# Weight splits and a scaling of X move from GpSimd to VectorE, and three groups of instructions are pinned in program order

## The chip, the cores and the metric

The kernel runs on one core of one Trainium2 chip. A core has TensorE (matmul, and its weight load), VectorE, ScalarE, GpSimd and SyncE; profiles call them PE and PEld, DVE, ACT, POOL and SP. The metric is the device time of one execution in microseconds, as the median of several runs; lower is better.

## The reference: what is computed

A sequence of 256 tokens of width 1024 goes through three transformer layers, all in float32:

```python
# layer 1: short convolution and gated linear attention, then a convolved gated MLP
x = x + rmsnorm(mixer(rmsnorm(x)) @ w_out);  x = x + rmsnorm(conv_mlp(rmsnorm(x)))
# layer 2: two kinds of attention, a SwiGLU, a per-layer gate
x = layer_norm(ALPHA * x + fox_sb_mixer(x));  x = layer_norm(ALPHA * x + swiglu(x))
x = x + sigmoid(x @ ple_gate[0]) * (p[0] @ ple_proj[0])
# layer 3: sliding-window attention, a mixture of experts, a per-layer gate
x = layer_norm(ALPHA * x + swa_mixer(x))
x = layer_norm(ALPHA * x + moe_swiglu(x))     # 8 experts, each token in its best 2
x = x + sigmoid(x @ ple_gate[1]) * (p[1] @ ple_proj[1])
```

The mixture computes router logits, takes the softmax of the two best, and adds up each expert's output with these weights. An expert has a 1024 x 7168 gate-and-up matrix and a 3584 x 1024 down matrix, 44 MB together, and the eight of them are most of what is read.

## The kernel before, in words

**Weights as a stream.** All weights are packed on the host into granules of 128 x 2048 float32 (1 MB), listed in the order of their use (`queue`, from L290), and loaded by SP into a ring of buffers called `raw`: 5 at first, 16 in the experts. The ring moves on when a granule is used up (`finish`, `load`). Some entries of the queue aren't weights: `("rep", 6)` holds the gain and the bias of the norm ahead of the experts, and while `main.hold` stands at its place in the queue, no buffer from that one on is loaded again.

**Splits.** For precision most weights are used as two fp32r parts. Each granule is split by halves of 128 x 1024 (`Stream.split`, L389): ScalarE rounds `raw` to `wh` (L405), and `wl = raw - wh` is done on VectorE (L409) or, for the halves named in `main.aside`, on GpSimd (L407). `ASIDE` (L31) names two halves behind each of six weight matrices: those are split while a norm is running. Three matmuls (`mm3`, L462 to L464) then make the product. Four halves can be live (`HALVES`), and splitting runs three halves ahead of use (`AHEAD`).

**The norms between the stages.** Each projection that ends a stage adds into `X` (tokens on partitions, two tiles `tt` of 128), takes the statistics, raises the variance to -1/2 on GpSimd (`rsqrt`, L617), and writes `X` in two halves `u`: L736 after the RMS norms of layer 1, L1062 and L1068 after a LayerNorm. Then TensorE turns `X` around (`turn_in`, L666) for the next stage. In a LayerNorm, `ordered[0]` makes `keep` pin what is traced between the first and the second token tile in program order, splits on VectorE among them.

**Who sets the order.** The program is traced in one order, and a scheduler then orders each engine's queue by its own estimate of when inputs are ready; `tc.keep_in_program_order(ins)` pins an instruction behind everything traced on its engine so far. `put_off` holds functions that are traced later: `flush_once` runs those waiting, and is called after each granule's matmuls, so that what is put off lands between two granules.

**The experts.** A router (L1557 to L1572) gives each token its places, `ranks` (L1584) each token's slot within an expert. `gates` (L1624) then computes the two gates of a token and calls `sort` (L1648), which orders the experts by their number of tokens and hands that order to SP as registers (L1669): in the order of the work, crowded experts alternate with those of few tokens. `in_order` puts the gates and slots into that order. `gates` also scales X by the gain and adds the bias, on GpSimd (L1644, L1645), and lets `main.hold` go. Expert 0 doesn't depend on the order. Its input comes from `gather` (L1707): matmuls of X with a one-hot of the slots (L1715), evacuated by ScalarE and VectorE by halves of four blocks (L1742, L1744) and split (L1745, L1746).

An expert's 3584 hidden columns go in seven blocks. `up(j)` takes four granules, `down(j - 1)` two, in turn. `Expert` works on 128 tokens with split weights, 12 matmuls a granule; `ExpertOfFew` on 64 with the weights as they are (L1791, L1823), which are neither rounded nor subtracted. There `gated` applies Silu and multiplies (L1799, L1800), and `turn` transposes the product (L1806) and copies it (L1808) for `down(j)`:

```python
                def turn():
                    pt = bank()
                    for m in range(2):
                        TE.transpose(pt[:, m * P:m * P + P], sg[:, m * P:m * P + P], ident)
                    ht = mh.tile([P, 2, P], F32, name="ht", tag="hh")
                    V.tensor_copy(ht, pt[:, :T].rearrange("p (a b) -> p a b", a=2))
```

In program order `gated` is traced behind the first granule of `down(j - 1)` and `turn` behind the second; in the last block of each half of the experts (`soon`) each is one granule earlier.

Of the kernel before, what the change touches and what calls it, by code (L numbers as in the profile page):

```python
# [28 lines left out]
GW = 2048  # L29

ASIDE = dict(w_out=(0, 2), w_down=(1, 3), ab_out=(0, 2), ffn_dn=(1, 3), c_out=(1, 2), moe=(0, 1))  # L31


# [190 lines left out]
def block_kernel(ctx: ExitStack, tc: tile.TileContext, A: dict, out: bass.AP):  # L224
# [94 lines left out]
    class Stream:  # L319
# [4 lines left out]
        def __init__(self, queue, pool, depth):  # L324
# [17 lines left out]
            self.fine = set()  # L342
            self.aside = set()

# [44 lines left out]
        def split(self, upto):  # L389
            while len(self.parts) < min(upto, self.stop):  # L390
                n = len(self.parts)
                i, h = self.halves[n]
                if i in self.as_is:
                    self.parts.append(None)
                    continue
                if self.live >= HALVES:
                    break
                self.live += 1
                self.load()
                hi = hlp.tile([P, GW // 2], F32R, name="wh")  # L400
                lo = hlp.tile([P, GW // 2], F32R, name="wl")
                step = GW // 8 if i in self.fine else GW // 2
                for c in range(0, GW // 2, step):
                    raw = self.raws[i][:, h * GW // 2 + c:h * GW // 2 + c + step]
                    S.activation(hi[:, c:c + step], raw, AF.Copy)  # L405
                    if n in self.aside:
                        nc.gpsimd.tensor_tensor(lo[:, c:c + step], raw, hi[:, c:c + step], op=ALU.subtract)  # L407
                    else:
                        keep(V.tensor_tensor(lo[:, c:c + step], raw, hi[:, c:c + step], op=ALU.subtract))  # L409
                self.parts.append((hi, lo))  # L410
                if n + 1 == len(self.halves) or self.halves[n + 1][0] != i:
                    self.finish(i)
                self.load()
# [36 lines left out]
    main = Stream(queue, rawp, RAW)  # L450
    for n, key in enumerate(queue[1:], 1):
        if queue[n - 1][0] != key[0] and queue[n - 1][0] in ASIDE and queue[n - 1][0] != "moe":
            main.aside |= {main.first[n] + i for i in ASIDE[queue[n - 1][0]]}
    main.fine |= {0, 1}
    main.aside |= {main.first[queue.index(("ple_p", 1))] + i for i in ASIDE["moe"]}
    stream = [main]
# [1164 lines left out]
    with tc.tile_pool(name="moe", bufs=1, side="right") as mp, tc.tile_pool(name="moe2", bufs=2, side="right") as mw, \  # L1621
            tc.tile_pool(name="moeh", bufs=2, side="right") as mh:
        Y = mp.tile([P, 2, D], F32, name="Y")
        def gates():  # L1624
            oh1, oh2, t8 = (mp.tile([P, 2, 8], F32, name=n) for n in ("oh1", "oh2", "t8"))
            m1, m2, ga = (mp.tile([P, 2, 1], F32, name=n) for n in ("m1", "m2", "ga"))
            for oh, m, n in ((oh1, m1, 0.0), (oh2, m2, 1.0)):
                V.tensor_scalar(oh, place, n, None, op0=ALU.is_equal)
                V.tensor_tensor(t8, oh, lg, op=ALU.mult)
# [12 lines left out]
            gain = main.other(("rep", 6)).rearrange("p (n d) -> p n d", n=2)  # L1642
            for tt in range(2):
                nc.gpsimd.tensor_tensor(X[:, tt], X[:, tt], gain[:, 0], op=ALU.mult)  # L1644
                nc.gpsimd.tensor_tensor(X[:, tt], X[:, tt], gain[:, 1], op=ALU.add)  # L1645
            main.hold = len(queue)

        def sort():  # L1648
# [5 lines left out]
            def by8(v):  # L1654
                return C(v).rearrange("p (a b) -> p a b", a=8)
            V.tensor_copy(t8, cnt)
            V.memset(t8[:, 0:1], 1000.0)
# [17 lines left out]
            V.tensor_copy(cnti, pos[:, 0:1])  # L1675
            V.tensor_scalar(slot, sel8, -1000.0, 1000.0, op0=ALU.mult, op1=ALU.add)
            V.tensor_tensor(slot, slot, rank, op=ALU.add)
# [79 lines left out]
        class ExpertOfFew:  # L1757
# [24 lines left out]
            def up(self, j, before=iter(()), soon=False):  # L1782
# [20 lines left out]
                def turn():  # L1803
                    pt = bank()
                    for m in range(2):
                        TE.transpose(pt[:, m * P:m * P + P], sg[:, m * P:m * P + P], ident)  # L1806
                    ht = mh.tile([P, 2, P], F32, name="ht", tag="hh")
# [266 lines left out]
```

## Time and profile before

| | |
|---|---|
| time, median of 3 runs | 1705.84 us (1705.81 to 1706.9) |
| profiled execution: its time | 1706.26 us |
| profiled execution: span of the trace | 1704.5 us, mean granted TensorE clock 0.985 |
| VectorE busy | 1065.2 us (62%), 1516 instructions |
| ScalarE busy | 841.1 us (49%), 1159 instructions |
| GpSimd busy | 52.9 us (3%), 36 instructions |
| DMA | 487.76 MB, mean 286 GB/s |

How to read it: a profile is of one execution, and its own time stands 1.76 us above its span, since the span runs from the first to the last instruction. Shares of busy time are means over stages that differ: the first 780 us are layers 1, 2 and the attention of layer 3, the experts run to about 1660 us, the rest is the last norm and gate. In a timeline a line merges neighbouring instructions of one kind (x4 is four of them), and the bracket at its end says how long the engine stood idle before it and what ended that.

### The profile page before, as it was taken

How to read it: one execution, taken by the hardware profiler on the slowest of the kernel's cores; microseconds unless marked ns; L12 is line 12 of the kernel's file. 1: busy time of each engine (PE TensorE's matmuls, PEld its weight loads, DVE VectorE, ACT ScalarE, POOL GpSimd, SP SyncE). 2: the span in 40 equal slices, each digit the busy share in tenths (PEclk: the TensorE clock that was granted, in tenths of full speed). 3: DMA queues.
4: the chain of work that ended last, by engine and by line, in shares of the span. 5: the costliest groups of instructions: out<-in, count | busy, mean ns of one | idle time of the engine just before them, and what ended most of it. 6: DMA issues, size and time to landing. Idle time of an engine off the chain costs nothing. (4 is left out here: it accounts for less than half of the span.)

```text
span 1704.5 us, 23510 instructions
## 1 busy us (share of the span) xinstructions
PE 1637.6 (96%) x9029; PEld 1223.9 (72%) x9029; DVE 1065.2 (62%) x1516; ACT 841.1 (49%) x1159; POOL 52.9 (3%) x36
## 2 busy tenths in 40 slices
PE   8999999899899999997999999999799999999997
PEld 7988998798699987966886357863378734787325
DVE  6578996566755557678996139961189712897107
ACT  7346665446454534564774037740177601686013
POOL 0000000100100001003000000000000000000001
PEclk9999999999999999997999999999999999999999
DMA  8344554543255554834998999999999899999990
GB/s 321 114 171 171 188 192 170 195 173 124 103 200 177 182 185 165 355 114 150 371 364 328 420 420 420 420 392 421 418 369 420 324 421 420 420 420 393 420 390 25
DMA packets 69668, 487.76 MB, mean 286 GB/s; under 512 B 7739, under 2 KB 8763, under 8 KB 11308
## 3 DMA queue, kind: packets, MB, share of 16 engines
q1 hardware_dynamic: 68572, 484.10, 72.1%
q10 hardware_dynamic: 896, 1.82, 0.3%
q8 instruction: 72, 1.18, 0.3%
q0 software_dynamic: 80, 0.26, 0.1%
q14 instruction: 48, 0.39, 0.1%
HBM read 485.11 MB, written 1.05 MB: 285 GB/s over the span
## 5 line engine op out<-in xcount | busy, mean ns | idle before, releaser
L409 DVE TENSOR_TENSOR wl<-raw,wh 128x1024 fp32r<-128x1024 f32 (+1 forms) x570 | 679.5, 1201 | 229.7 <-ACT wh L405 224.3
L405 ACT ACTIVATE wh<-raw 128x1024 fp32r<-128x1024 f32 (+1 forms) x582 | 602.5, 1042 | 360.9 <-PE mm L464 176.7
L462 PE MATMUL mm<-a_l,wh 128*128 128x256 f32 x1008 | 284.5, 283 | 0.0
L463 PE MATMUL mm<-a_h,wh 128*128 128x256 f32 x1008 | 281.4, 279 | 0.0
L464 PE MATMUL mm<-a_h,wl 128*128 128x256 f32 x1008 | 281.1, 279 | 0.0
L1791 PE MATMUL mm<-raw,xgf 128*64 128x512 f32 x896 | 200.4, 595 | 0.0
L462 PEld LDWEIGHTS mm<-a_l,wh 128*128 128x128 f32 x1008 | 189.3, 188 | 2.8 <-issue 1.7
L463 PEld LDWEIGHTS mm<-a_h,wh 128*128 128x128 f32 x1008 | 188.9, 187 | 0.7 <-issue 0.5
L464 PEld LDWEIGHTS mm<-a_h,wl 128*128 128x128 f32 x1008 | 189.1, 188 | 0.0
L462 PE MATMUL mm<-wl,xg 128*128 128x512 f32 x448 | 181.4, 405 | 6.5 <-ACT xg L1745 6.5
L464 PE MATMUL mm<-wh,xg 128*128 128x512 f32 x448 | 177.2, 396 | 0.9 <-DVE xg L1746 0.9
L463 PE MATMUL mm<-wh,xg 128*128 128x512 f32 x448 | 177.6, 396 | 0.0
L1791 PEld LDWEIGHTS mm<-raw,xgf 128*64 128x64 f32 x896 | 62.1, 137 | 118.9 <-issue 117.2
L598 ACT ACTIVATE sgf<-mm 128x256 f32<-128x256 f32 x28 | 10.7, 384 | 234.4 <-PE mm L1791 234.4
L1800 DVE TENSOR_TENSOR sgf<-sgf,mm 128x256 f32<-128x256 f32 x28 | 11.8, 420 | 176.5 <-ACT sgf L598 176.5
L462 PEld LDWEIGHTS mm<-wl,xg 128*128 128x128 f32 x448 | 84.5, 189 | 28.6 <-ACT xg L1745 6.7
L1823 PE MATMUL at<-raw,ht 128*64 128x512 f32 x448 | 102.5, 598 | 0.0
L464 PEld LDWEIGHTS mm<-wh,xg 128*128 128x128 f32 x448 | 84.3, 188 | 21.7 <-DVE xg L1746 1.1
L463 PEld LDWEIGHTS mm<-wh,xg 128*128 128x128 f32 x448 | 84.6, 189 | 18.7
L463 PE MATMUL at<-wh,hh 128*128 128x512 f32 x224 | 89.1, 398 | 0.0
L462 PE MATMUL at<-wl,hh 128*128 128x512 f32 x224 | 89.1, 398 | 0.0
L464 PE MATMUL at<-wh,hl 128*128 128x512 f32 x224 | 87.9, 393 | 0.0
(409 smaller groups left out, 2071.8 us busy)
## 6 DMA issues: line engine op xcount, KB each, us to landing
raw<-in_moe_gu_dram SPq DMA_DIRECT2D x224, 1024.0 KB, 12.4
raw<-in_moe_dn_dram SPq DMA_DIRECT2D x112, 1024.0 KB, 12.5
raw<-in_w_up_dram SPq DMA_DIRECT2D x22, 1024.0 KB, 4.8
raw<-in_ffn_gu_dram SPq DMA_DIRECT2D x22, 1024.0 KB, 4.8
raw<-in_w_in_dram SPq DMA_DIRECT2D x12, 1024.0 KB, 10.5
raw<-in_ab_in_dram SPq DMA_DIRECT2D x12, 1024.0 KB, 4.8
raw<-in_w_down_dram SPq DMA_DIRECT2D x10, 1024.0 KB, 4.8
raw<-in_ffn_dn_dram SPq DMA_DIRECT2D x10, 1024.0 KB, 4.8
```

What stands on the lines that cost most here:

```text
L405: S.activation(hi[:, c:c + step], raw, AF.Copy)
L409: keep(V.tensor_tensor(lo[:, c:c + step], raw, hi[:, c:c + step], op=ALU.subtract))
L462: TE.matmul(o, lh, rl, start=start, stop=False)
L463: TE.matmul(o, lh, rh, start=False, stop=False)
L464: TE.matmul(o, ll, rh, start=False, stop=stop)
L598: latest[:] = [S.activation(*args, **kw)]
L1791: TE.matmul(ps[rows_of(t)], self.xg[:, k], w[:, t * 512:t * 512 + 512], start=(k == 0), stop=(k == NB - 1), skip_group_check=True)
L1800: tc.keep_in_program_order(V.tensor_tensor(sg, sg, ps[:, T:], op=ALU.mult))
L1823: TE.matmul(self.py[rows_of(s)], self.hts[j][:, m, rows_of(t)], w[:, s * 512:s * 512 + 512], start=(j == 0 and t == m == 0), stop=(j == 6 ...
```

## The change

It does four things. `ASIDE` and `main.aside` go, so all splits are done by VectorE (L409). The scaling of X by gain and bias goes from four GpSimd instructions in `gates` to four on VectorE, each put off by one flush from the one before; `main.hold` is let go with the last. The first instructions of `gates`, of `sort` and of the slots' order are pinned in program order on VectorE, so that they stand behind what is traced before them, the gather of expert 0 and its evacuation included. The transposes of a few-token expert are pinned in program order on TensorE.

```diff
@@ -27,9 +27,6 @@
 ALPHA = 4.0 ** 0.25
 NEG = -1.0e30
 GW = 2048
-
-ASIDE = dict(w_out=(0, 2), w_down=(1, 3), ab_out=(0, 2), ffn_dn=(1, 3), c_out=(1, 2), moe=(0, 1))
-
 
 
 
@@ -340,7 +337,6 @@
             self.cap = len(queue)
             self.stop = len(self.halves)
             self.fine = set()
-            self.aside = set()
 
         def pool_of(self, i):
             if self.turn is None or i < self.turn[0]:
@@ -403,10 +399,7 @@
                 for c in range(0, GW // 2, step):
                     raw = self.raws[i][:, h * GW // 2 + c:h * GW // 2 + c + step]
                     S.activation(hi[:, c:c + step], raw, AF.Copy)
-                    if n in self.aside:
-                        nc.gpsimd.tensor_tensor(lo[:, c:c + step], raw, hi[:, c:c + step], op=ALU.subtract)
-                    else:
-                        keep(V.tensor_tensor(lo[:, c:c + step], raw, hi[:, c:c + step], op=ALU.subtract))
+                    keep(V.tensor_tensor(lo[:, c:c + step], raw, hi[:, c:c + step], op=ALU.subtract))
                 self.parts.append((hi, lo))
                 if n + 1 == len(self.halves) or self.halves[n + 1][0] != i:
                     self.finish(i)
@@ -448,11 +441,7 @@
         return tc.keep_in_program_order(ins) if ordered[0] else ins
 
     main = Stream(queue, rawp, RAW)
-    for n, key in enumerate(queue[1:], 1):
-        if queue[n - 1][0] != key[0] and queue[n - 1][0] in ASIDE and queue[n - 1][0] != "moe":
-            main.aside |= {main.first[n] + i for i in ASIDE[queue[n - 1][0]]}
     main.fine |= {0, 1}
-    main.aside |= {main.first[queue.index(("ple_p", 1))] + i for i in ASIDE["moe"]}
     stream = [main]
 
     def granule(key):
@@ -1625,7 +1614,7 @@
             oh1, oh2, t8 = (mp.tile([P, 2, 8], F32, name=n) for n in ("oh1", "oh2", "t8"))
             m1, m2, ga = (mp.tile([P, 2, 1], F32, name=n) for n in ("m1", "m2", "ga"))
             for oh, m, n in ((oh1, m1, 0.0), (oh2, m2, 1.0)):
-                V.tensor_scalar(oh, place, n, None, op0=ALU.is_equal)
+                tc.keep_in_program_order(V.tensor_scalar(oh, place, n, None, op0=ALU.is_equal))
                 V.tensor_tensor(t8, oh, lg, op=ALU.mult)
                 V.tensor_reduce(m, t8, axis=AX.X, op=ALU.add)
             V.tensor_tensor(m2, m2, m1, op=ALU.subtract)
@@ -1640,10 +1629,15 @@
             sort()
             in_order(comb_w, comb)
             gain = main.other(("rep", 6)).rearrange("p (n d) -> p n d", n=2)
-            for tt in range(2):
-                nc.gpsimd.tensor_tensor(X[:, tt], X[:, tt], gain[:, 0], op=ALU.mult)
-                nc.gpsimd.tensor_tensor(X[:, tt], X[:, tt], gain[:, 1], op=ALU.add)
-            main.hold = len(queue)
+
+            def gains(n):
+                tt, op = n // 2, (ALU.mult, ALU.add)[n % 2]
+                tc.keep_in_program_order(V.tensor_tensor(X[:, tt], X[:, tt], gain[:, n % 2], op=op))
+                if n < 3:
+                    put_off.append(lambda: gains(n + 1))
+                else:
+                    main.hold = len(queue)
+            put_off.append(lambda: gains(0))
 
         def sort():
 
@@ -1653,7 +1647,7 @@
 
             def by8(v):
                 return C(v).rearrange("p (a b) -> p a b", a=8)
-            V.tensor_copy(t8, cnt)
+            tc.keep_in_program_order(V.tensor_copy(t8, cnt))
             V.memset(t8[:, 0:1], 1000.0)
             other, own = t8.unsqueeze(1).to_broadcast([P, 8, 8]), t8.unsqueeze(2).to_broadcast([P, 8, 8])
             V.tensor_tensor(lt, other, own, op=ALU.is_lt)
@@ -1673,7 +1667,7 @@
             V.tensor_reduce(pos[:, 0:1], t8, axis=AX.X, op=ALU.max)
             V.tensor_scalar(pos[:, 0:1], pos[:, 0:1], 0.0, None, op0=ALU.max)
             V.tensor_copy(cnti, pos[:, 0:1])
-            V.tensor_scalar(slot, sel8, -1000.0, 1000.0, op0=ALU.mult, op1=ALU.add)
+            tc.keep_in_program_order(V.tensor_scalar(slot, sel8, -1000.0, 1000.0, op0=ALU.mult, op1=ALU.add))
             V.tensor_tensor(slot, slot, rank, op=ALU.add)
             in_order(slot_w, slot)
 
@@ -1803,7 +1797,7 @@
                 def turn():
                     pt = bank()
                     for m in range(2):
-                        TE.transpose(pt[:, m * P:m * P + P], sg[:, m * P:m * P + P], ident)
+                        tc.keep_in_program_order(TE.transpose(pt[:, m * P:m * P + P], sg[:, m * P:m * P + P], ident))
                     ht = mh.tile([P, 2, P], F32, name="ht", tag="hh")
                     V.tensor_copy(ht, pt[:, :T].rearrange("p (a b) -> p a b", a=2))
                     self.hts.append(ht)
```

## Rows read from the trace of the kernel before

**Rows 1.** Page, busy time of each engine, its share of the span, instructions.

```profile
PE 1637.6 (96%) x9029; PEld 1223.9 (72%) x9029; DVE 1065.2 (62%) x1516; ACT 841.1 (49%) x1159; POOL 52.9 (3%) x36
```

**Rows 2.** Waits of TensorE, whole span: us in total, times, longest us.

```profile
PE at L1806 <- DVE sgf L1800: 13.2, 14, 0.9
PE xT L666 <- DVE X L1068: 12.0, 5, 3.3
PE xT L666 <- DVE X L736: 7.2, 6, 2.3
...
PE mm L462 <- ACT xg L1745: 6.5, 1, 6.5
...
PE mm L462 <- POOL wl L407: 1.4, 1, 1.4
```

**Rows 3.** Groups by line, whole span: splits on VectorE and on GpSimd.

```profile
L409 DVE TENSOR_TENSOR wl<-raw,wh 128x1024 fp32r<-128x1024 f32 (+1 forms) x570 | 679.5, 1201 | 229.7 <-ACT wh L405 224.3 <-ACT xg L1745 1.3 <-DMA raw<-in_moe_dn_dram 0.2
...
L407 POOL TENSOR_TENSOR wl<-raw,wh 128x1024 fp32r<-128x1024 f32 x12 | 30.4, 2543 | 866.9 <-ACT wh L405 866.9
```

**Rows 4.** VectorE's instructions on X: min/median/max ns, first to last start.

```profile
L736 DVE SCALAR_TENSOR_TENSOR X<-y,post_y,X x8: 739/753/2848, 125.2 to 331.6; 128x512 f32<-128x512 f32 x8
...
L1068 DVE SCALAR_TENSOR_TENSOR X<-X,ln_y,gb x8: 744/1789/2865, 452.8 to 661.3; 128x512 f32<-128x512 f32 x8
```

**Rows 5.** Timeline, 446 to 470 us: start, us, engine, line, operation.

```profile
452.63 5.24 POOL L407 TENSOR_TENSOR wl<-raw,wh 128x1024 fp32r<-128x1024 f32 x2
452.82 5.60 DVE L1068 SCALAR_TENSOR_TENSOR X<-X,ln_y,gb 128x512 f32<-128x512 f32 x2
...
455.81 0.63 PE L666 MATMUL xT<-cst_all,X 128*128 128x128 f32 x4 [2.57 <-DVE X L1068]
...
466.84 1.41 DVE L1068 SCALAR_TENSOR_TENSOR X<-X,ln_y,gb 128x512 f32<-128x512 f32 x2
```

**Rows 6.** Windows: us; PE, PEld, DVE, ACT, POOL busy; PEclk, DMA share, GB/s.

```profile
456.00:464.00 8.00, 5.88 (x20) 4.71 (x19) 7.46 (x8) 2.25 (x3) 1.87 (x1) 0.57 0.11 15
...
656.00:664.00 8.00, 8.00 (x26) 6.38 (x25) 7.19 (x12) 2.82 (x5) 0.92 (x1) 0.66 0.70 228
```

**Rows 7.** Timeline of TensorE in two few-token experts, 910 to 1240 us.

```profile
956.93 7.09 PE L1791 MATMUL mm<-raw,xgf 128*64 128x512 f32 x32
...
967.75 7.09 PE L1791 MATMUL mm<-raw,xgf 128*64 128x512 f32 x32
...
1178.86 0.44 PE L1806 MATMUL at<-cst_all,sgf 128*128 128x128 f32 x2 [0.94 <-DVE sgf L1800]
...
1190.68 0.44 PE L1806 MATMUL at<-cst_all,sgf 128*128 128x128 f32 x2 [0.94 <-DVE sgf L1800]
```

**Rows 8.** Last few-token expert: windows, SP's issues, TensorE's last L1823.

```profile
1650.00:1655.00 5.00, 4.06 (x20) 1.26 (x18) 1.45 (x3) 2.19 (x3) 0.00 (x0) 1.00 1.03 426
1655.00:1660.00 5.00, 5.00 (x26) 1.58 (x22) 0.00 (x0) 0.00 (x0) 0.00 (x0) 1.00 0.77 318
...
1635.01 12.16 SPq L369 DMA_DIRECT2D raw<-in_ple_g_dram  x4
...
1653.26 7.09 PE L1823 MATMUL at<-raw,ht 128*64 128x512 f32 x32
```

**Rows 9.** Timeline around the start of expert 0, 762 to 812 us.

```profile
775.12 2.17 DVE L1571 TENSOR_SCALAR selb<-place 128x8 bf16<-128x8 f32 x1
...
784.44 0.17 DVE L1571 TENSOR_SCALAR selb<-place 128x8 bf16<-128x8 f32 x1
...
785.69 1.99 DVE L1579 TENSOR_SCALAR oh<-cst_moe,rank,sel 128x128 f32<-128x128 f32 x1
...
794.05 2.38 DVE L1665 TENSOR_TENSOR rt_gt<-perm,cst_moe 128x64 f32<-128x64 f32 x1
...
798.03 0.80 PE L462 MATMUL mm<-wl,xg 128*128 128x512 f32 x1 [6.47 <-ACT xg L1745]
```

**Rows 10.** Window in the middle of expert 0, columns as in rows 6.

```profile
875.00:900.00 25.00, 25.00 (x113) 20.17 (x112) 23.04 (x22) 20.11 (x22) 0.00 (x0) 1.00 0.97 360
```

## The prediction

> **What bounds the kernel now.** I read the page first, then TensorE's waits, then GpSimd's groups, then the timeline wherever a wait and a GpSimd instruction meet, and last the windows for the clock and the DMA. TensorE is busy 96% of the span [rows 1], so only the time in which it stands still, or runs at half clock, can be won. Its waits [rows 2] fall into three families: 14 waits of about 0.9 us on the gated product of a few-token expert (13.2 us), 11 waits on the two VectorE lines that write X at the end of a norm (12.0 and 7.2 us), and one of 6.5 us ahead of the first expert.
>
> **Why the norms are late.** GpSimd's twelve splits take 2.54 us each against VectorE's 1.20 [rows 3], but the larger cost is beside them. L1068 takes 0.74 us at its shortest, 1.79 at the median and 2.87 at the longest; L736 goes from 0.74 to 2.85 [rows 4]. The timeline says why: at 452.63 two GpSimd splits run back to back for 5.24 us, and the pair of L1068 that starts beside them needs 5.60 us; the same pair at 466.84, with GpSimd idle, needs 1.41 [rows 5]. So a VectorE instruction with its operands in SBUF stands still until the GpSimd one ends: 4.2 us lost there, and TensorE waits 2.57 us for it at 455.81. Behind such waits the clock falls: 0.57 of full speed granted in 456 to 464, 0.66 in 656 to 664 [rows 6], which means that half clock (1.2 GHz) was granted for much of each stretch.
>
> **The change, part by part.**
>
> *Few-token transposes (L1806).* In a block where the two transposes stand behind the preceding block's 16 L1823 matmuls, the period is 967.75 - 956.93 = 10.82 us; where they come before these, it is 1190.68 - 1178.86 = 11.82, with an idle 0.94 in it [rows 7]. Pinning turns the second order into the first: 1.0 us in each of 14 places [rows 2], **14.0 us**. The pin adds a wait in TensorE's queue, with the next block queued behind it, but what it waits for is ready some 0.9 us after the last L1791 and is covered by 16 L1823, 3.5 us by the 32 that take 7.09 [rows 8]; in the last block of a half eight of these (1.8 us) still cover it. If the cover were gone, the 0.9 would be back. The copy of the transposes (L1808) is due only a block later.
> Can the weights keep up? DMA is saturated in the last few-token expert: 426 GB/s in 1650 to 1655, then 318 in 1655 to 1660, so it ends near 1658.8. Four 1 MB loads of ple_g are issued behind the last expert weight, about 10 us at 426 GB/s; that weight was therefore in by 1649 and is read near 1658.4, in the last quarter of the 32 matmuls at 1653.26 [rows 8]. At least 9 us of lead, and an expert with its seven blocks gives back 7 us at the most: TensorE stays the bound. Bounds 12 to 14.2.
>
> *Twelve splits go to VectorE.* Added there: 12 x 1.20 = 14.4 us [rows 3]. Removed: up to 2.1 us of standing still for each instruction caught beside a GpSimd one [rows 4]. After the LayerNorms (L1068), the splits traced between the two token tiles are kept in program order, so they line up behind X; there TensorE gets X as soon as 0.74 us permits. Of 12.0 us of wait I take **7.5 us** back (lower bound 4, if splits that weren't kept in order come first, upper 11). After the RMS norms (L736) nothing keeps the order, and a split of 1.20 us may come between the two halves of X: 7.2 us of wait, less 1.2 in about three places, is **3.5 us** (1.5 to 6). The 1.4 us that TensorE waits for a GpSimd split in the last stage [rows 2] may become 0.2, or the split may push the last norm by 1.2: counted at nothing, from -1.2 to +1.2. ACT's part of a split is not touched. GpSimd keeps the powers of the norms, which now find an empty queue; its one DMA isn't near them.
>
> *The clock behind these waits.* A stretch of 8 us at 0.57 and one at 0.66 lose at most 0.43 x 8 + 0.34 x 8 = 6.2 us [rows 6]; of that some 1.6 lies in the waits already counted. If the waits shrink to under a microsecond I expect full clock: **4 us** (0 to 4.6).
>
> *Start of the experts.* Before: the route of the first tile stands 2.17 us in L1571, which takes 0.17 when GpSimd is idle; the slots of the second tile (L1579), which the gather's last 16 matmuls wait for, take 1.99; and the evacuation is stuck on VectorE among the ordering's instructions, one of which (L1665) takes 2.38, so the first expert matmul starts at 798.03 after 6.47 us of idle [rows 9]. After: L1571 gives 2.0 us, less a split of 1.2 in its place, so 0.8; L1579 gives about 1.7 (0.3 left, by the 0.17 of L1571 with a wider output: an estimate); and the evacuation, ahead of the ordering, needs about a microsecond instead of 6.47, giving 5.5. The start is 8 us earlier.
> Then VectorE pays. The ordering and the gates are some 40 small instructions, at 0.17 us [rows 9] 6.8 us, now behind the split of the fifth half and beside the splits that TensorE needs; four scalings of X, 128x1024 like a split, add 4 x 1.20 = 4.8. Part of the 6.8 ran beside expert 0 already. In a dense expert VectorE is busy 23.04 of 25 us [rows 10], so it has 8% free; 113 matmuls in 25 us are 0.22 each, six to a half, so a split is due three halves, 4.0 us, after its buffer comes free; VectorE's 1.20 and about as much on ACT leave some 1.5 us of lead. Of 11.6 us the lead takes 1.5, the free share over 30 us 2.4, and what ran there before about 4: some 3.5 us of TensorE stalls remain. Net **4.5 us**; bounds 8 + 2 = 10 (no stall, splits out of the way) and 8 - 11.6 = -3.6.
> Two queues are passed. SP reads the expert order into registers, and the loads behind that wait with it; the release of the slot that holds the gains (main.hold) comes four flushes later, near 4 x 2.8 us. Both are hidden by the weights already loaded: 16 buffers of two halves are 32 x 6 x 0.22 = 42 us of TensorE's work. Should they take longer, expert 0 would starve.
>
> **The sum.** 14.0 + 7.5 + 3.5 + 4 + 4.5 = 33.5 us. The profiled execution took 1706.26 us, 1.76 outside its span; 1706.26 - 33.5 = **1672.8 us**. The median of three is 1705.84, 0.4 lower, well inside the uncertainty.
>
> **Rivals.**
> 1. *VectorE becomes the bound at the boundaries and in expert 0.* Twelve splits, four scalings and the ordering sit on one in-order queue. Then the start nets -3.6 instead of 4.5, and the norms give 4 and 1.5 instead of 7.5 and 3.5: 33.5 - 8.1 - 5.5 = 19.9, so 1686 us. For: 23.04 of 25. Against: VectorE's total falls, since each of the slowed instructions loses more than a split costs. The Trainium skill's page Perfetto Trace Analysis (Optimizing Scalar/DVE Operations) says that with a saturated VectorE, moving work to GpSimd may pay, adding that the two share a read port and it might not; by its first half this rival is what the change gets, by its second the sum above, and the 5.60 against 1.41 us agrees with the second.
> 2. *The bubbles stay or turn into another wait* (weights not there, or the pin doesn't bring the transposes behind the L1823): 14 us less, 1687 us. For: DMA is saturated in these stretches. Against: the 9 us of lead, and the blocks of 10.82 that the kernel already has.
> 3. *Slower.* L1068's and L736's long times have another cause than GpSimd, and stay; then VectorE does 16 x 1.20 = 19.2 us more right where TensorE waits for it, against the 14 of the transposes: 5 us slower, 1711 us. It decides if L1068 beside no GpSimd instruction still takes over 1.9 us (0.74 + 1.20). The pair of 1.41 speaks against it.
>
> **How the numbers follow.** Forecast 70%, rival 1 14%, rival 2 11%, rival 3 5%. Time 1672.8 us. All lower bounds at once give 12 + 4 + 1.5 + 0 - 3.6 - 1.2 = 12.7, so 1694; all upper ones 14.2 + 11 + 6 + 4.6 + 10 + 1.2 = 47, so 1659; both rivals that are still faster end at 1687, so I take 1661 to 1690. A measurement of this kernel tells about 0.2% (3.4 us) from no change: faster 0.92, within it 0.03, slower 0.05.
>
> **What would show it.** Right: no wait L1806 on L1800, few-token periods of 10.8 us throughout; L1068 and L736 near 0.74 us everywhere; waits of L666 together under 8 us; full clock around the earlier 456 and 656 us; the first L462 of expert 0 about 8 us earlier, with a few stalls of L462 on VectorE's wl in the 30 us behind it. Wrong: waits of TensorE on L409 of tens of microseconds, few-token blocks that wait for a DMA, or L1068 still long.

## The result, and the profile after

The changed kernel takes **1680.89 us** (median of 4 runs, 1680.42 to 1682.12) against 1705.82 (4 runs, 1705.49 to 1706.9) of the kernel before on the same chip: ratio 0.9854, 95% interval 0.9837 to 0.9871. It is 24.9 us faster, where 33.5 were forecast; the time lies in the range of 1661 to 1690. The profiled execution took 1682.12 us, its span is 1680.3.

First the page of the changed kernel, its busy times and the group of all splits on VectorE (rows 1 and 3 of before).

```profile
PE 1632.1 (97%) x9029; PEld 1218.1 (72%) x9029; DVE 1054.3 (63%) x1532; ACT 840.3 (50%) x1159; POOL 16.0 (1%) x20
...
L402 DVE TENSOR_TENSOR wl<-raw,wh 128x1024 fp32r<-128x1024 f32 (+1 forms) x582 | 693.6, 1202 | 224.3 <-ACT wh L401 220.6
```

VectorE now does all 582 splits, at 1202 ns on the mean. It has 16 instructions more (12 splits and 4 scalings) and is busy 10.9 us less than in [rows 1]: what it no longer spends standing still is more than the work that it took over, some 16 x 1.2 = 19 us.

TensorE's waits in the changed kernel, whole span: us in total, times, longest us (rows 2 of before).

```profile
PE mm L451 <- DVE wl L402: 8.5, 5, 4.8
PE xgp L1709 <- DVE oh L1684: 7.0, 1, 7.0
PE at L451 <- DVE a_l L682: 6.4, 1, 6.4
PE at L1870 <- DVE comb_w L1679: 6.0, 1, 6.0
PE mm L1577 <- DVE selb L1560: 3.0, 1, 3.0
PE mm L451 <- ACT xg L1739: 1.9, 1, 1.9
...
PE xT L655 <- DVE X L1057: 1.5, 2, 1.2
...
PE xT L655 <- DVE X L725: 1.1, 3, 0.4
```

The three families of [rows 2] are gone or small: no wait of the few-token transposes (13.2 before), 1.5 and 1.1 us on the lines that write X (12.0 and 7.2 before), 1.9 on xg (6.5 before). Two large waits are new: 8.5 us on the splits, with one of 4.8 in it, and 6.0 us of `L1870` on comb_w, the gates in the order of the experts. The largest of the other new ones is 1.7 us, in the last stage. The waits of 7.0, 6.4 and 3.0 us were there before, at 7.0, 6.1 and 2.8.

VectorE's instructions on X in the changed kernel: min/median/max ns, first and last start (rows 4 of before).

```profile
L725 DVE SCALAR_TENSOR_TENSOR X<-y,post_y,X x8: 743/750/753, 126.4 to 327.1; 128x512 f32<-128x512 f32 x8
...
L1057 DVE SCALAR_TENSOR_TENSOR X<-X,ln_y,gb x8: 743/746/750, 448.2 to 651.4; 128x512 f32<-128x512 f32 x8
```

All of them now take 0.74 to 0.75 us, where [rows 4] had up to 2.87.

Windows of the changed kernel around the norms that had lost clock in [rows 6]; columns as there.

```profile
120.00:140.00 20.00, 18.19 (x85) 13.94 (x84) 14.89 (x31) 12.26 (x31) 2.16 (x3) 1.00 0.48 172
440.00:470.00 30.00, 26.76 (x127) 20.59 (x127) 24.51 (x36) 12.59 (x17) 1.96 (x2) 1.00 0.44 158
640.00:670.00 30.00, 29.77 (x139) 23.48 (x139) 24.71 (x36) 16.68 (x22) 1.83 (x2) 1.00 0.54 197
```

The granted clock is 1.00 in all three; the kernel before had 0.91, 0.89 and 0.89 in the same windows.

TensorE's timeline in a few-token expert of the changed kernel (rows 7 of before).

```profile
935.14 7.09 PE L1785 MATMUL mm<-raw,xgf 128*64 128x512 f32 x32
942.06 3.60 PE L1817 MATMUL at<-raw,ht 128*64 128x512 f32 x16
945.60 0.44 PE L1800 MATMUL at<-cst_all,sgf 128*128 128x128 f32 x2
945.96 7.09 PE L1785 MATMUL mm<-raw,xgf 128*64 128x512 f32 x32
```

The transposes stand behind the 16 matmuls of the preceding block, and the period is 945.96 - 935.14 = 10.82 us, as forecast.

**Where the time went.** I cut every trace at four instructions of TensorE that all kernels have: the first router matmul, the first product of expert 0, the first product of the first few-token expert, and the end of the last few-token down product. These are the rows of the changed kernel (timeline of TensorE; the last one ends at 1628.51 + 5.37 = 1633.88):

```profile
753.71 0.97 PE L1541 MATMUL mm<-wrg,xT 128*128 128x8 f32 x8
...
777.59 0.50 PE L451 MATMUL mm<-wl,xg 128*128 128x512 f32 x1 [1.93 <-ACT xg L1739]
...
907.83 1.51 PE L1785 MATMUL mm<-raw,xgf 128*64 128x512 f32 x6
...
1628.51 5.37 PE L1817 MATMUL at<-raw,ht 128*64 128x512 f32 x24
```

In the kernel before they are at 768.03, 798.03 [rows 9], 918.80 and 1660.34 (the end of the last row of matmuls in [rows 8]). The first line of the table has the five stages of that kernel in us, the others what each kernel's stages take more (+) or less (-). The names of the experiments are explained below. Each line is one execution. The granted clock of a stretch differs a little between executions (from 0 to 200 us it was 0.99 in the kernel before and 1.00 in p4_turns), and a stage differs by up to 2.5 us where nothing in it was changed (p4_turns and p3_pins ahead of the router): single figures below that say little.

| kernel | layers to router | router to expert 0 | expert 0 | experts 1 to 7 | last norm and gate | sum |
|---|---|---|---|---|---|---|
| before, us | 768.0 | 30.0 | 120.8 | 741.5 | 44.2 | 1704.5 |
| **after** | -14.3 | -6.1 | **+9.5** | -15.5 | +2.3 | -24.2 |
| p1_splits | -14.6 | +1.5 | +0.7 | -0.9 | +2.4 | -10.8 |
| p2_scale | -0.2 | -6.3 | +1.8 | +2.8 | -0.1 | -2.0 |
| p3_pins | +2.1 | -4.3 | **+7.4** | -0.9 | -1.1 | +3.2 |
| p4_turns | -2.5 | -0.9 | +1.2 | -14.0 | -0.4 | -16.6 |
| e_late | -15.3 | -4.5 | +4.4 | -14.4 | +1.3 | -28.6 |
| u_nopins | -14.6 | -6.0 | +0.5 | -14.5 | +1.3 | -33.3 |
| k_pin_gates | -14.2 | -6.8 | +0.6 | -14.4 | +1.2 | -33.6 |
| j_nopins_pool | -15.1 | +1.2 | +0.3 | -15.2 | +2.6 | -26.2 |
| g_last_pool | -13.8 | -6.1 | +9.4 | -13.5 | -0.2 | -24.2 |
| h_both | -15.3 | -4.5 | +4.3 | -14.5 | -0.2 | -30.1 |
| i_nopins_last | -15.3 | -6.5 | +0.5 | -14.8 | -0.2 | -36.3 |

The line of the changed kernel says where the forecast and the result part: the norms ahead of the router, the earlier start and the transposes gave what was forecast of them, within 2 us each, but expert 0 took 9.5 us more, and the last stage 2.3.

### The profile page after: what moved, and what is told of

The parts are those of the page before. It is cut to its first block, busy times and chain, and to the rows that moved or that the text cites. A ratio compares the mean times of both kernels' runs of the same rounds, so it can differ in the third digit from the quotient of the medians.

```text
span 1680.3 us, 23507 instructions
## 1 busy us (share of the span) xinstructions
PE 1632.1 (97%) x9029; PEld 1218.1 (72%) x9029; DVE 1054.3 (63%) x1532; ACT 840.3 (50%) x1159; POOL 16.0 (1%) x20
## 5 line engine op out<-in xcount | busy, mean ns | idle before, releaser
L402 DVE TENSOR_TENSOR wl<-raw,wh 128x1024 fp32r<-128x1024 f32 (+1 forms) x582 | 693.6, 1202 | 224.3 <-ACT wh L401 220.6
## 6 DMA issues: line engine op xcount, KB each, us to landing
raw<-in_moe_dn_dram SPq DMA_DIRECT2D x112, 1024.0 KB, 14.4
```

## The experiments

**One part of the change at a time.** Four kernels make one part each on the kernel before. They ran on one chip, where the kernel before took 1706.93 us (21 runs, 1699.06 to 1710.39).

*p1_splits: all splits on VectorE.*

```diff
-                    if n in self.aside:
-                        nc.gpsimd.tensor_tensor(lo[:, c:c + step], raw, hi[:, c:c + step], op=ALU.subtract)
-                    else:
-                        keep(V.tensor_tensor(lo[:, c:c + step], raw, hi[:, c:c + step], op=ALU.subtract))
+                    keep(V.tensor_tensor(lo[:, c:c + step], raw, hi[:, c:c + step], op=ALU.subtract))
```

> The kernel before with the weight splits alone taken off GpSimd. In the trace of the whole change TensorE has won 14.4 us by the time it reaches the last attention, and it has lost 2.7 between the last expert and the end, where it now waits 4.8 us for a VectorE split. Theory: both belong to the splits, so this part alone gives about 12 us, 1694 us, with X at the norms back near 0.74 us an instruction and that wait of 4.8 us present. Rival: the norms became shorter for another reason (a different order of the queue); then under 4 us are won, and L736 and L1068 stay long.

Measured: 1694.4 us, ratio 0.9934 (0.9911 to 0.9957). TensorE's waits in its trace, up to the router (0 to 754 us):

```profile
PE mm L459 <- DVE wl L406: 3.0, 3, 1.6
PE xT L663 <- DVE X L1065: 1.5, 2, 1.2
PE xT L663 <- DVE X L733: 1.1, 3, 0.4
```

In the kernel before, the two waits on X come to 8.6 and 7.2 us in that stretch. So 13.2 us of wait go, 3.0 come on VectorE's splits, and the stage is 14.6 us shorter. The splits are the cause of the first column, all of it; in the last column they cost 2.4 us.

*p2_scale: the scaling of X on VectorE, put off granule by granule.*

```diff
-            for tt in range(2):
-                nc.gpsimd.tensor_tensor(X[:, tt], X[:, tt], gain[:, 0], op=ALU.mult)
-                nc.gpsimd.tensor_tensor(X[:, tt], X[:, tt], gain[:, 1], op=ALU.add)
-            main.hold = len(queue)
+            def gains(n):
+                tt, op = n // 2, (ALU.mult, ALU.add)[n % 2]
+                tc.keep_in_program_order(V.tensor_tensor(X[:, tt], X[:, tt], gain[:, n % 2], op=op))
...
+            put_off.append(lambda: gains(0))
```

> The kernel before with the four scalings of X alone moved to VectorE, each put off by a flush. Theory: the four VectorE instructions that stood 2.0 to 2.4 us beside GpSimd ones ahead of expert 0 become short, the start comes 4 to 7 us earlier, and the 4.8 us of scalings cost 0 to 3 us of stalls in expert 0: 1700 to 1703 us. Rival (VectorE has no room there): the stalls take back all, 1705 us or more.

Measured: 1704.94 us, 0.9988 (0.9972 to 1.0005), not to be told from no change. Its waits:

```profile
PE at L1810 <- DVE sgf L1804: 15.0, 16, 0.9
...
PE mm L462 <- ACT xg L1749: 1.8, 1, 1.8
```

The wait on xg falls from 6.5 to 1.8 us, and the stage ahead of expert 0 is 6.3 us shorter. But in this program the scheduler put two more of the few-token transposes ahead of their cover (16 waits of 0.9 instead of 14), and expert 0 takes 1.8 us more, of which the trace shows 0.7 as waits on VectorE's splits. The time lies between the theory's range and the rival's.

*p3_pins: the three places on VectorE kept in program order.*

```diff
-                V.tensor_scalar(oh, place, n, None, op0=ALU.is_equal)
+                tc.keep_in_program_order(V.tensor_scalar(oh, place, n, None, op0=ALU.is_equal))
...
-            V.tensor_copy(t8, cnt)
+            tc.keep_in_program_order(V.tensor_copy(t8, cnt))
...
-            V.tensor_scalar(slot, sel8, -1000.0, 1000.0, op0=ALU.mult, op1=ALU.add)
+            tc.keep_in_program_order(V.tensor_scalar(slot, sel8, -1000.0, 1000.0, op0=ALU.mult, op1=ALU.add))
```

> The kernel before with the three pins on VectorE alone (gates, order of the experts, slots); scaling and twelve splits stay on GpSimd. Theory: the pins bring the evacuation forward by about 5 us, but the chain of small instructions that ends in comb_w then runs between the splits of expert 0, and the product with comb_w (L1876), which keeps its place in TensorE's queue, waits for it by 4 to 8 us: in all between 2 us faster and 5 us slower, 1704 to 1711 us. Rival: the wait on comb_w in the changed kernel comes from the four scalings on VectorE; then there is none here, and the time is about 1701 us.

Measured: 1709.0 us, 1.0009 (0.9994 to 1.0025): nothing gained. The start is 4.3 us earlier, the wait on xg falls to 1.8 us, and expert 0 takes 7.4 us more, with a wait that the kernel before hasn't:

```profile
PE at L1876 <- DVE comb_w L1685: 4.6, 1, 4.6
```

*p4_turns: the few-token transposes kept in program order.*

```diff
-                        TE.transpose(pt[:, m * P:m * P + P], sg[:, m * P:m * P + P], ident)
+                        tc.keep_in_program_order(TE.transpose(pt[:, m * P:m * P + P], sg[:, m * P:m * P + P], ident))
```

> The kernel before with the few-token transposes alone pinned. Theory: each of the 14 places gives 1.0 us, so 1692 us, with every few-token period near 10.8 us and no new wait. Rival: the weights can't keep up, or what is won is lost again at the next expert; then 1698 us or more, with waits of TensorE for a DMA.

Measured: 1691.73 us, 0.9917 (0.9889 to 0.9945); 14.0 us less in experts 1 to 7, the wait of 13.2 us gone, no other in its place. Medians put the four parts at -12.5, -2.0, +2.1 and -15.2 us against 1706.93, together -27.6; by the ratios -11.3, -2.0, +1.5 and -14.2, together -26.0; the whole change gives -24.9. So the parts add up within the scatter, as a total. By stages two of them overlap: the scaling alone and the kept places alone start expert 0 earlier by 6.3 and 4.3 us, all parts together by 6.1. The part to look at is the third.

**Why expert 0 is slow.** The kept places were to bring the evacuation of expert 0's input ahead of the ordering. VectorE's timeline of the changed kernel, at both ends of what then follows:

```profile
781.53 0.17 DVE L1617 TENSOR_SCALAR oh<-place 128x16 f32<-128x16 f32 x1
781.73 0.17 DVE L1618 TENSOR_TENSOR t<-oh,lg 128x16 f32<-128x16 f32 x1
781.82 1.22 DVE L402 TENSOR_TENSOR wl<-raw,wh 128x1024 fp32r<-128x1024 f32 x1
782.96 0.16 DVE L1619 TENSOR_REDUCE m<-t 128x2 f32<-128x16 f32 x1
...
805.82 0.17 DVE L1667 TENSOR_REDUCE pos<-t8b 128x1 f32<-128x8 f32 x1
805.89 1.23 DVE L402 TENSOR_TENSOR wl<-raw,wh 128x1024 fp32r<-128x1024 f32 x1
...
809.50 0.22 DVE L1679 TENSOR_REDUCE comb_w<-rt_ge 128x8 f32<-128x64 f32 x1
```

And TensorE's timeline there:

```profile
809.35 0.56 PE L1870 MATMUL at<-comb_w,oh 128*128 128x1 f32 x2 [6.03 <-DVE comb_w L1679]
```

These are 40 small instructions of 0.06 to 0.23 us, most of which need the one before. The scheduler put 19 splits and scalings of 1.2 us between them, and VectorE takes its queue in order, so the chain from 781.53 to 809.72 lasts 28.2 us. TensorE reaches `L1870`, which the scheduler had placed by its own estimate for comb_w, 6.03 us too early. The matmuls behind it wait too, although VectorE had ended the last split ahead of it at 807.12.

Two kernels take that apart. *u_nopins* drops the three kept places, and nothing else. *e_late* moves the call `ex.gates()` to the fourth block of expert 0. Its expectation takes that for the gates and the ordering, but the call is the method of `Expert`, which turns the one-hot of the slots around and makes the product with comb_w (`L1870`): what moves is TensorE's instruction that waits, and the function `gates` with the ordering on VectorE stays where it was. These two, g_last_pool and h_both ran on one chip, where the kernel before took 1708.01 us (9 runs, 1703.52 to 1710.93); so the ratios are what to compare. First the edit of e_late:

```diff
-                ex.gates()
+                if wait is None or before is not None:
+                    ex.gates()
...
+                    if j == 3 and wait is not None and before is None:
+                        ex.gates()
```

> The changed kernel, with the gates and the ordering of the experts issued in the fourth block of expert 0 (j = 3) instead of behind its first up block. Theory (the three kept vector operations put the chain of gates and ordering between the splits of expert 0's first block, so that it takes 28 us, and TensorE runs into the slot_gates product that waits 6.0 us for comb_w, with the clock at half behind it): later in expert 0 the splits have run ahead and nothing of TensorE's is queued behind comb_w yet, so the 6.0 us wait is gone or under 1 us, the half-clock stretch of 6.8 us behind it (some 3.4 us of work lost) too; 1672 to 1676 us, ratio to the kernel before 0.980 to 0.983. Rival (the chain is long wherever it stands, because each of its some 40 small operations waits for a split of 1.2 us to end): a wait of 3 to 7 us for comb_w or for the weights' low halves shows later in expert 0, and the time stays at 1679 to 1682 (0.984 to 0.986).

Measured: 1675.66 us, 0.981 (0.9794 to 0.9826). The wait on comb_w is not in its list, and expert 0 takes 5.1 us less than in the changed kernel. The two ends of the chain in VectorE's timeline of e_late:

```profile
783.41 0.17 DVE L1617 TENSOR_SCALAR oh<-place 128x16 f32<-128x16 f32 x1
...
821.90 0.20 DVE L1679 TENSOR_REDUCE comb_w<-rt_ge 128x8 f32<-128x64 f32 x1
```

And the product that waited, in TensorE's timeline:

```profile
835.92 0.50 PE L1870 MATMUL at<-comb_w,oh 128*128 128x1 f32 x4
```

The chain starts behind the evacuation as before and lasts 38.7 us, longer than the 28.2 of the changed kernel, and costs no wait, since TensorE comes to `L1870` only 13.8 us after its end. Theory and rival both supposed a chain that moves, so neither was put to the test as worded. What the run shows is that a late chain alone does not stop TensorE; an instruction in TensorE's queue that waits for it does. What e_late keeps of the loss goes mostly with the clock: its trace has 0.50 of full speed (1.2 GHz) granted from 774 to 784 us, where the changed kernel has 1.00, and expert 0 begins in that stretch, at 778.2; some 6 us at half clock are 3 of the 4.4 us. Three short waits of 0.8, 0.6 and 0.2 us in expert 0, which the changed kernel has too, come to 1.6. Why the clock came back later there is open.

The edit of u_nopins:

```diff
-                tc.keep_in_program_order(V.tensor_scalar(oh, place, n, None, op0=ALU.is_equal))
+                V.tensor_scalar(oh, place, n, None, op0=ALU.is_equal)
...
-            tc.keep_in_program_order(V.tensor_copy(t8, cnt))
+            V.tensor_copy(t8, cnt)
...
-            tc.keep_in_program_order(V.tensor_scalar(slot, sel8, -1000.0, 1000.0, op0=ALU.mult, op1=ALU.add))
+            V.tensor_scalar(slot, sel8, -1000.0, 1000.0, op0=ALU.mult, op1=ALU.add)
```

> The changed kernel without the three kept vector operations (one-hot oh, t8, slot); splits and scaling of X stay on VectorE, few-token transposes stay kept. Theory (the kept operations are what puts TensorE's wait of 6.0 us for comb_w there): the wait is gone, as in the kernel before, and with it the half clock behind it; what the kept operations were to take away comes back, a wait of some 6.5 us of the first product of expert 0 for the gathered xg instead of 1.9. Net 1676 to 1679 us, ratio 0.982 to 0.984. Rival (the wait comes of the four scaling operations and the additional splits on VectorE, not of the kept ones): a wait of 4 us or more for comb_w stays, the xg wait comes on top, and the time is 1681 to 1687 (0.985 to 0.989).

Measured: 1673.01 us, **0.9797** (0.9778 to 0.9817), better than my theory had it. Expert 0 is back to +0.5 us, and the wait on xg did not come back. VectorE's timeline of u_nopins:

```profile
775.52 0.22 DVE L1678 TENSOR_TENSOR rt_ge<-perm,slot 128x64 f32<-128x64 f32 x1
...
775.99 0.72 DVE L1736 TENSOR_SCALAR v<-xgp,small 128x128 f32<-128x128 f32 x2
...
785.20 0.21 DVE L1679 TENSOR_REDUCE comb_w<-rt_ge 128x8 f32<-128x64 f32 x1
```

And its first product of expert 0, in TensorE's timeline:

```profile
777.45 0.50 PE L451 MATMUL mm<-wl,xg 128*128 128x512 f32 x1 [2.05 <-ACT xg L1739]
```

Most of the ordering runs between 773 and 779 us, before and between the evacuations (`L1736`), while VectorE would wait for the gather, at 0.2 us an instruction; comb_w is done at 785.4 instead of 809.7. The same window holds the place of the wait in the changed kernel and is full in u_nopins; columns as in [rows 6]. First u_nopins:

```profile
800.00:815.00 15.00, 15.00 (x68) 12.07 (x68) 14.46 (x15) 11.79 (x13) 0.00 (x0) 1.00 1.01 405
```

And the changed kernel:

```profile
800.00:815.00 15.00, 8.97 (x32) 7.05 (x31) 10.56 (x30) 4.92 (x7) 0.71 (x1) 0.77 0.63 254
```

Of 15 us, 6.0 are the wait. The granted clock of 0.77 is not all lost work, because the half clock begins inside the wait, where TensorE has nothing to do (0.56 was granted in 807 to 808 us). Behind the wait the changed kernel has:

```profile
809.35:814.50 5.15, 5.15 (x15) 4.29 (x16) 1.02 (x5) 1.52 (x3) 0.16 (x1) 0.55 0.98 387
```

That is 0.45 x 5.15 = 2.3 us of lost work. With the wait of 6.0, and 1.6 us of short waits in expert 0 where u_nopins has 0.9, it makes 9.0 us, which is what expert 0 takes more than in u_nopins (+9.5 against +0.5).

*k_pin_gates* asks how much of the chain it takes: it keeps only the place in the gates (`L1617`), the ordering is free. It ran on one chip with j_nopins_pool and i_nopins_last, the kernel before at 1706.45 us (9 runs, 1703.61 to 1708.34).

```diff
-            tc.keep_in_program_order(V.tensor_copy(t8, cnt))
+            V.tensor_copy(t8, cnt)
...
-            tc.keep_in_program_order(V.tensor_scalar(slot, sel8, -1000.0, 1000.0, op0=ALU.mult, op1=ALU.add))
+            V.tensor_scalar(slot, sel8, -1000.0, 1000.0, op0=ALU.mult, op1=ALU.add)
```

> The changed kernel with the kept order at L1617 alone (the two one-hot operations of the gates); the copy at L1650 and the slot operation at L1670, which begin the ordering, are free again. Theory (the wait for comb_w comes of the length of the chain: each small operation behind the evacuation waits out one split of 1.2 us, and all three kept places together put some 32 of them there): the ordering, 17 operations, runs early again, 14 are left behind the evacuation, at 1.2 us each some 17 us from 781, so comb_w is there by about 798, when TensorE has its first block still to do; no wait above 1 us for comb_w, no half clock there, ratio to before within 0.0015 of the version without kept operations (0.9797), some 1672 to 1676 us. Rival (one kept operation is enough, since what follows it in the program is held with it): a wait of 3 us or more for comb_w, half clock behind it, ratio 0.983 to 0.986.

Measured: 1673.28 us, 0.9812 (0.9798 to 0.9825), no wait for comb_w. Its chain, from VectorE's timeline:

```profile
780.96 0.17 DVE L1617 TENSOR_SCALAR oh<-place 128x16 f32<-128x16 f32 x1
...
796.80 0.21 DVE L1679 TENSOR_REDUCE comb_w<-rt_ge 128x8 f32<-128x64 f32 x1
```

17 small instructions instead of 40, 16 us instead of 28, still with splits between them; it ends at 797.01, and TensorE starts `L1870` at 797.43. So what counts is the end of the chain against the place of `L1870`: 16 us are just short enough for it, and the two kept places in the ordering made the chain too long; in e_late a longer one did no harm behind a later `L1870`.

**What the start of the experts owes to which part.** In u_nopins the start stays early without the kept places. *j_nopins_pool* puts the scaling back on GpSimd in that kernel.

```diff
-            put_off.append(lambda: gains(0))
+            for tt in range(2):
+                nc.gpsimd.tensor_tensor(X[:, tt], X[:, tt], gain[:, 0], op=ALU.mult)
+                nc.gpsimd.tensor_tensor(X[:, tt], X[:, tt], gain[:, 1], op=ALU.add)
+            main.hold = len(queue)
```

> The changed kernel without the three kept operations and with the scaling of X on GpSimd again. Theory (the 4.5 us that I predicted for the start of the experts do come, and come from the scaling's move off GpSimd alone, because VectorE's small operations at the start of expert 0 no longer stand still for some 2 us each): expert 0's first product waits some 6.5 us for xg instead of 2.0, three or more small operations of 2.0 to 2.4 us are back, and the time is 3 to 6 us above the version without kept operations: ratio 0.9815 to 0.983. Rival (four operations of 1.2 us on VectorE in its full stretch cost as much as they free): ratio 0.979 to 0.981.

Measured: 1680.06 us, 0.9847 (0.9833 to 0.986), somewhat more than the theory's 0.9815 to 0.983. The first two of GpSimd's scalings in its timeline:

```profile
771.58 2.34 POOL L1634 TENSOR_TENSOR X<-X,raw 128x1024 f32<-128x1024 f32 x1 [6.89 <-PE mm L1582]
774.00 2.37 POOL L1635 TENSOR_TENSOR X<-X,raw 128x1024 f32<-128x1024 f32 x1
```

VectorE's instructions beside them, in its timeline:

```profile
771.74 2.26 DVE L1568 TENSOR_SCALAR oh<-cst_moe,rank,sel 128x128 f32<-128x128 f32 x1
...
774.07 2.33 DVE L1667 TENSOR_TENSOR slot<-slot,rank 128x16 f32<-128x16 f32 x1
```

And, among TensorE's waits:

```profile
PE mm L451 <- ACT xg L1735: 6.3, 1, 6.3
```

Beside each of the four scalings one instruction of VectorE lasts until the scaling ends (2.26, 2.33, 2.06 and 2.17 us): the first takes 0.35 us at this line in the changed kernel, the second works on 16 columns. The way from the router to expert 0 is 7.2 us longer than in u_nopins (+1.2 against -6.0). So without the kept places the whole gain at the start belongs to the scaling's move. It is not the only way to it: with the scaling on GpSimd the kept places alone brought 4.3 us (p3_pins); on top of the scaling's move they add nothing (6.1 against 6.0).

**The last stage.** *g_last_pool* and *h_both* put two of the twelve splits back on GpSimd, those ahead of the last norm: the first in the changed kernel, the second in e_late, so that h_both, too, moves `L1870` and not the ordering.

```diff
+                    if n in self.aside:
+                        nc.gpsimd.tensor_tensor(lo[:, c:c + step], raw, hi[:, c:c + step], op=ALU.subtract)
+                    else:
...
+    main.aside |= {main.first[queue.index(("ple_p", 1))] + i for i in (0, 1)}
```

> The changed kernel with two of the last stage's low halves (halves 0 and 1 of ple_p) subtracted on GpSimd again, as in the kernel before; all other splits stay on VectorE. Theory (in the last stage VectorE's two splits of 2.35 us stand inside the last norm, and the 4.8 us wait for wl is theirs): that wait falls under 1 us, a wait for GpSimd's halves of some 1.4 us and the old wait of the last transposes for X of some 3 us come back, the GpSimd power of the norm goes from 3.2 us back to some 1 us; net gain 1 to 3 us, 1678 to 1680, ratio 0.983 to 0.985. Rival (the two ways cost the same, as my prediction had it, within 1 us): 1680 to 1682 (0.9845 to 0.986), with the waits of the last stage adding up to the same.

> The two edits together: gates and ordering of the experts in the fourth block of expert 0, and two low halves of the last stage's ple_p on GpSimd. Theory (two losses at two places, independent): gains add up, 1670 to 1675 us, ratio 0.978 to 0.982, faster than both kernels. Rival (either gain is taken back, the first by a new wait for comb_w later in expert 0, the second by the transposes' wait for X): no better than the better of the two alone, 1676 to 1681 (0.983 to 0.986).

Measured: g_last_pool 1681.05 us, 0.9842 (0.9827 to 0.9858); h_both 1674.63, 0.98 (0.9783 to 0.9818). By the times alone neither is to be told from the kernel that it was made from. In the traces the last stage is 46.4 us in the changed kernel and 44.0 in g_last_pool, 45.4 in e_late and 44.0 in h_both. TensorE's waits from 1620 us on, in the changed kernel:

```profile
PE mm L451 <- DVE wl L402: 4.8, 1, 4.8
PE mm L451 <- ACT raw L1078: 1.7, 1, 1.7
```

And in g_last_pool:

```profile
PE xT L660 <- DVE X L1062: 3.3, 1, 3.3
PE mm L456 <- POOL wl L404: 1.4, 1, 1.4
```

That is 6.5 against 4.7 us; each has one more of 0.7. With all splits on VectorE, two pairs of them, 2.35 us each, come into the first token tile's norm, at 1640.11 and 1643.10 us; with two on GpSimd, the norm's last pair takes 3.49 us.

*i_nopins_last* joins what helped: no kept places on VectorE, and these two splits on GpSimd; both edits are shown above.

> The changed kernel without the three kept operations and with two of the last stage's low halves on GpSimd. Theory (two losses at two places): the last stage gives back some 2 us, as from the version with the late gates to the one with both edits, where the trace's end came 1.9 us earlier: 1669 to 1672 us, ratio 0.977 to 0.979, the fastest of all. Rival (the last stage costs the same either way, the wait of 4.8 us for wl against 3.3 for X and 1.4 for GpSimd's half): no difference to the version without kept operations, ratio 0.979 to 0.981.

Measured: 1669.98 us, **0.9784** (0.9768 to 0.9799), the fastest kernel of this study, 0.7% below the changed kernel by the ratios, whose intervals don't meet. Against u_nopins its last stage is 1.5 us shorter. The gain of the last stage has one sign in three pairs of traces (2.4, 1.4 and 1.5 us) but is within the scatter of the times.

## Why the prediction was right, and where it failed

- **Few-token transposes, 14.0 us: right.** 14.0 us alone (p4_turns), 15.5 in the whole change, which is above the bound of 14.2, but the kernels made from it show 13.5 to 15.2 with the same transposes; period 10.82; no wait on weights appeared. Rival 2 falls.
- **Twelve splits, 7.5 + 3.5 us, and the clock, 4 us: right in sum.** Ahead of the router 14.3 us went, the splits alone gave 14.6 (p1_splits). The waits on X fell from 15.8 to 2.6 us there; new waits of 3.0 us on splits and 0.6 on the residue of an input leave 9.6. The remaining 4.7 I put on the clock, which no run varies by itself: the granted clock rose from 0.91, 0.89 and 0.89 to 1.00 in the windows shown above, at most 0.09 x 20 + 2 x 0.11 x 30 = 8.4 us of work, some of it within waits already counted. I had 11 and 4, with the last norm's part in the 11. L1068's successor at 0.75 us everywhere rules out rival 3, which needed it above 1.9.
- **The last stage, counted at nothing: wrong by 2.3 us**, outside its bounds of -1.2 to +1.2. I had a single split of 1.2 us delay the norm; two pairs of splits come in between, and TensorE waits 4.8 us for the first of them. The wait on GpSimd's half that I wanted to save was 1.4.
- **Start of the experts, +4.5 us net: the step that failed.** It came out at -6.1 + 9.5 = 3.4 us of loss, 7.9 off, most of the 8.6 between forecast and result. Its first half was 8 us of earlier start: 6.1 came, and the runs put it on another part than I did. I gave 5.5 of it to the evacuation's place ahead of the ordering, which the kept places secure. They do bring it forward while the scaling is on GpSimd (4.3 us in p3_pins), but with the scaling moved the start is as early without them (24.0 us from router to expert 0 against 23.9), since beside an idle GpSimd the ordering takes so little that it is not in the way. Its second half, "VectorE then pays", priced the ordering as 6.8 us of work against VectorE's free share (11.6 - 1.5 - 2.4 - 4 is 3.7 us of stalls, put down as 3.5). The price is not work but latency: 40 small instructions, most of them dependent, with 19 long ones between them last 28 us on an in-order engine, and TensorE has a matmul for their result in its own queue, which waits 6.0 us and is followed by 2.3 us lost to half clock; with that matmul moved back, the chain stays long and the wait is gone (e_late). I had named the wait for weights (3.5 us) and looked for nothing else that waits for the ordering but SP.
- **Rival 1** had the place (expert 0, the ordering on VectorE's one queue) and the size of the stage, 3.6 us lost against 3.4, but not the mechanism: TensorE waited 0.6 us for a split in expert 0, against 6.0 for comb_w. Its other half, splits in the way at the norms, came in the last norm alone. The Trainium skill's page PSUM — Partial Sum Buffer (Engine vs sequencer instructions) calls VectorE's queue a strict FIFO, and this trace agrees: the chain's instruction at 782.96, whose input was ready at 781.90, starts within 0.1 us of the end of the split of 781.82.
- **Without the kept places in the ordering the total of the forecast comes out**: u_nopins 0.9797 x 1705.82 = 1671.2 us, k_pin_gates 0.9812 x 1705.82 = 1673.8, against 1672.8. That is partly luck: the forecast was for the kernel with them, and its 5.5 us for the evacuation's place are not what u_nopins gains.
- **The range held partly by luck, too**: the start was 7.9 us worse than forecast and the last stage 2.3, and only the transposes, 1.5 us better, set anything against them; no term forecast for the start had the right cause for the loss.

## What to carry to other kernels

Price a chain of small dependent instructions on a shared in-order engine by what the scheduler may put between them, link by link, and not by its own busy time; then look through every engine's queue for what waits at its end, since moving that back can help as much as shortening the chain (e_late). An instruction kept in program order keeps all that depends on it late as well: pin as little as brings the order that is wanted, and try the change without each pin. Moving work off GpSimd was worth more than its own time where VectorE runs small instructions on the critical path beside it: one of them stood still until each scaling on GpSimd ended, 2.06 to 2.33 us.

## What was unexpected of the hardware

The contention between the two engines goes the other way, too. GpSimd's power on 128x1 takes 0.54 us at its shortest, but in the last norm of the changed kernel, beside VectorE's splits, 3.20. GpSimd's timeline of the changed kernel:

```profile
1642.68 3.20 POOL L606 TENSOR_TENSOR ln_y<-ln_y,minus_half 128x1 f32<-128x1 f32 x1 [833.17 <-DVE ln_y L605]
```

The same power in g_last_pool, where no split of VectorE runs beside it:

```profile
1642.82 0.94 POOL L611 TENSOR_TENSOR ln_y<-ln_y,minus_half 128x1 f32<-128x1 f32 x1 [2.48 <-DVE ln_y L610]
```

The Trainium skill's page SBUF — State Buffer (Who interferes with whom) has it that the order of issue decides which of the two blocks; that agrees in so far as either engine was seen to lose, but the order itself is not shown here: an instruction of VectorE on X stands ahead of the power, at 1642.45, and the splits behind its start, at 1643.10. Here it cost nothing, since VectorE came to the instruction that uses the power only at 1646.04, behind the splits.
